# Block sums on VectorE and P1 and P2 of four column blocks ahead of the gate-up loop

## The chip, the cores and the metric

The kernel runs on one core of a Trainium2 chip. The core has a TensorE (matmuls), a VectorE, a ScalarE, a GpSimd and a SyncE (which here only issues DMAs); each runs its own instructions in order and waits for the others by semaphores. Activations and weights lie in SBUF (128 partitions), products are accumulated in PSUM. The metric is the device time of one execution in microseconds, median of several runs, lower is better.

## The reference

One encoder layer on a sequence of 1024 rows of 1024 elements, in float32: a half step of a gated feed-forward block, a mixer (latent attention and retention), and a second half step of feed-forward. The change lies in the feed-forward block alone:

```python
h = h + 0.5 * swiglu(rms_norm(h, ffn1_norm), ffn1_w_gate, ffn1_w_up, ffn1_w_down)
...                                              # mixer: attention and retention
h = h + 0.5 * swiglu(rms_norm(h, ffn2_norm), ffn2_w_gate, ffn2_w_up, ffn2_w_down)

def swiglu(x, w_gate, w_up, w_down):
    return (jax.nn.silu(x @ w_gate) * (x @ w_up)) @ w_down     # 1024 -> 2816 -> 1024
```

## The kernel before

A float32 product is made of three fast matmuls: every operand is split into a rounded part (ScalarE, a cast, line 75) and the rest (VectorE, a subtraction, line 79). `split` does both, so each operand costs one instruction on ScalarE and one on VectorE.

Each feed-forward block (`ffn`) has two stages. `gate_up` makes, for 22 blocks of 128 hidden columns (f = 0 to 21), the gate and up products. The 1024x1024 input is treated as a 2x2 matrix of blocks, and seven products in place of eight are formed from sums of blocks (Strassen's method in Winograd's form): P1 to P7, in the code `p1` to `p7`. One product is 12 matmuls of 128x512 on line 292. The inputs X of the products are six sums or blocks of the normed rows plus block 22 ("11", "21", "t2", "t3", "t1", "t4", "22"); they are made once per feed-forward block: `stats` squares rows on ScalarE and takes the reciprocal root in small steps on VectorE (lines 91 to 105), `scale` scales a row tile on VectorE (line 430), differences of rows are formed (line 456), and `turn` transposes 128x128 blocks on TensorE (line 435) and splits the result into X. The weight operands are a11, a12, a22 (raw blocks) and four sums s1 to s4, formed by `combine` and `combine4` (lines 272 to 278) on GpSimd from the raw gate and up blocks, which `fetch` brings into a ring of three raw buffers; `convert` splits an operand into one of the buffers of the pool "gu".

P1 and P2 of a block share a PSUM bank: P1 is copied out, then P2 is added to it and ScalarE takes SiLU of the sum. P6, P7, P5, P4 and P3 add further products to that; after P3 the hidden block is complete and `store` writes it to HBM. `hidden_sums` forms on GpSimd the block sums of two hidden blocks for the next stage, `fetch_down` and `down_sums` those of the down weights (through the tile "early", which holds P1 and P2 of the first blocks at the start).

Before the loop, the code is placed by a scheduler, which orders each engine's instructions by its own cost estimates; blocks 0 and 1 are done there, mixed with the transposes. From block 2 on, a hand-written list `steps` rules (`manual_schedule`): in each step one product, the conversion of the operand two steps ahead, and fetches and stores tied to certain steps. In steady state the order of a block is P7, P2, P5, P1 of the next block, P4, P6 of the next block, P3.

`down` (lines 559 to 685) runs seven passes of 11 groups of 12 matmuls (line 599) over the hidden sums and the down sums that lie in HBM; each step loads two 256 KB pieces (lines 581 and 587) and splits them (`operands`). What `gate_up` leaves over (`rest`: the last hidden block and its sums) is stored in the first pass after group 2, and the residual rows are loaded into `h` in the first pass from group 3 on. In the first feed-forward block, code that makes tables for the mixer (`tables`, from line 702) is placed by the scheduler near the end of `gate_up` and in the first pass of `down`.

Of the kernel before, what the change touches and what calls it, by code (L numbers as in the profile page):

```python
# [21 lines left out]
P = 128  # L22
# [39 lines left out]
class Layer:  # L62
# [181 lines left out]
    def gate_up(self, ctx, gain, wg, wu, wd, first):  # L244
        nc, tc, v = self.nc, self.tc, self.nc.vector
        HF = S // 2

# [19 lines left out]
        def combine(f):  # L267
# [3 lines left out]
            tt = nc.gpsimd.tensor_tensor  # L271
# [4 lines left out]
        def combine4(f):  # L276
            s = sums[f]
            nc.gpsimd.tensor_tensor(out=s[4], in0=raws["g", f][:, h2], in1=s[2], op=ALU.subtract)
# [31 lines left out]
        def p1(f):  # L310
            banks[f] = [self.ps.tile([P, HF], F32, name="dn")]
            product(banks[f][0], f, "a11", "11", True)
            kept[f, "p1"] = (early[:, 2 * f] if f < 2 else
                             take("p1"))
            nc.scalar.copy(out=kept[f, "p1"], in_=banks[f][0])  # L315

        def p2(f):
            product(banks[f][0], f, "a12", "21", False)
            kept[f, "gate1"] = (early[:, 2 * f + 1] if f < 2 else
# [56 lines left out]
        def fetch_down(m):  # L376
            b = kept["down"] = epool.tile([P, 4, 512], F32, name="early")
# [4 lines left out]
        def down_sums(m):  # L382

            b = kept.pop("down")
# [19 lines left out]
        with tc.tile_pool(name="gbc", bufs=2, reuse_waits="tile") as gpool:  # L404
            if first:
                self.load_x(1, 4)
            gbc = self.gain_rows(gpool, gain[0])
            fetch("g", 0)
            fetch("u", 0)
# [5 lines left out]
            fetch("g", 1)  # L415
# [22 lines left out]

            convert(0, "a11")
            convert(0, "a12")  # L440
            for c in range(2):
                stats(2 * c, 2)
                for t in (2 * c, 2 * c + 1):
                    scale(t)
                    turn("11", t, self.h[:, t, h1])
            for t in range(4):
                turn("21", t, self.h[:, t, h2])
            p1(0)
            combine(0)
            combine4(0)  # L450
            stats(4, 4)
            p2(0)
            convert(1, "a11")
            convert(1, "a12")

            tt = lambda eng, o, a, b: eng.tensor_tensor(out=o, in0=a, in1=b, op=ALU.subtract)
            t2s = {}
            for t in range(4):
                lo, hi = self.h[:, t], self.h[:, t + 4]
                scale(t + 4)  # L460
                t2s[t] = gpool.tile([P, 512], F32, name="t2", bufs=4)
                tt(v, lo[:, h1], hi[:, h1], lo[:, h1])
                tt(v, t2s[t], hi[:, h2], lo[:, h1])
                turn("t2", t, t2s[t])
                tt(nc.gpsimd, hi[:, h1], hi[:, h2], hi[:, h1])
                tt(nc.gpsimd, lo[:, h2], lo[:, h2], t2s[t])
            p1(1)
            for k in (2, 3):
                convert(0, k)
            for t in range(4):  # L470
                turn("t3", t, self.h[:, t + 4, h1])
            p2(1)
            p6(0)
            for t in range(4):
                turn("t1", t, self.h[:, t, h1])
            p7(0)
            for k in (1, "a22"):
                convert(0, k)
            fetch("u", 1)
            for t in range(4):  # L480
                turn("t4", t, self.h[:, t, h2])
            p5(0)
            convert(0, 4)
            combine(1)
            combine4(1)
# [3 lines left out]
        p4(0)  # L489
        p3(0)[0]()  # L490

        fetch("g", 2)
        store(0)
        convert(1, 2)
        fetch("u", 2)
        convert(1, 3)
        p6(1)
        p7(1)  # L500
        convert(1, 1)
        convert(1, "a22")
        p5(1)
        convert(1, 4)
        p4(1)
        combine(2)
        combine4(2)
        p3(1)[0]()
        fetch("g", 3)
        steps = [(p1, 2, "a11"), (p6, 2, 2)]  # L510
        for f in range(2, NF):
# [1150 lines left out]
```

## Time and profile before

| what | value |
|---|---|
| time, median of 3 runs | 2101.58 us (2097.86 to 2101.75) |
| profiled execution, its own time | 2099.66 us |
| its span from first to last instruction | 2097.4 us |
| mean granted TensorE clock | 0.979 |
| TensorE matmul busy | 1995.1 us (95%) |
| VectorE busy | 1312.0 us (63%) |
| ScalarE busy | 816.8 us (39%) |
| GpSimd busy | 747.7 us (36%) |

Shares are means over the whole span; a stage can have another limit than the mean shows. A stretch of the trace gives the busy time of each engine, the granted clock (1.00 is 2.4 GHz, 0.50 is 1.2 GHz) and the DMA share. The first feed-forward block (FFN1) begins with the execution and its `gate_up` ends near 489 us; the second (FFN2) begins near 1405 us and its `gate_up` ends near 1872 us.

### The profile page before, as it was taken

Reading aid. Unit: us, or ns where it says so; the run is one execution under the profiler, and the core shown is the slowest. Engines: PE = TensorE matmul, PEld = TensorE weight load, DVE = VectorE, ACT = ScalarE, POOL = GpSimd, SP = SyncE. Lnnn points to the kernel's source line nnn. Section 1 sums busy time; section 2 is a strip of 40 time slices with the busy share of each in tenths; the row PEclk is TensorE's granted clock in tenths of the full one; section 3 lists DMA queues with packets and bytes.
Section 4 is the critical chain, followed back from the end, with each engine's and each line's share of the span. In section 5 each row is a group of like instructions: output and inputs, shape, how many; then the busy total and the mean of one; then the engine's idle time right before and its main releaser. Section 6 shows DMA issues by size and latency. Waiting matters only on the chain. (4 is left out here: it accounts for less than half of the span.)

```text
span 2097.4 us, 28702 instructions
## 1 busy us (share of the span) xinstructions
PE 1995.1 (95%) x10776; PEld 1710.8 (82%) x10776; DVE 1312.0 (63%) x2000; ACT 816.8 (39%) x1424; POOL 747.7 (36%) x654
## 2 busy tenths in 40 slices
PE   4999999998999799999999999997999999999997
PEld 3778888886888699998878888995878888878876
DVE  8556665666555644526888888448566566565566
ACT  4322223224434331236567776224222322234444
POOL 4166666561210103312431110014376655641112
PEclk9899999999999899999999999998999999999999
DMA  4155454457666211110100000131345445468773
GB/s 150 35 167 171 161 170 150 147 170 244 232 192 191 83 41 42 51 31 1 45 12 1 1 1 21 41 131 31 134 151 173 153 148 181 146 213 283 221 229 112
DMA packets 201018, 254.66 MB, mean 121 GB/s; under 512 B 14000, under 2 KB 117680, under 8 KB 200880
## 3 DMA queue, kind: packets, MB, share of 16 engines
q1 hardware_dynamic: 199728, 250.74, 36.4%
q8 instruction: 85, 1.39, 0.3%
q10 hardware_dynamic: 1152, 2.10, 0.3%
q14 instruction: 53, 0.43, 0.1%
HBM read 180.96 MB, written 71.83 MB: 121 GB/s over the span
## 5 line engine op out<-in xcount | busy, mean ns | idle before, releaser
L292 PE MATMUL mm<-xt,gu 128*128 128x512 f32 x1584 | 387.0, 392 | 5.5 <-DVE tab L706 3.5
L292 PEld LDWEIGHTS mm<-xt,gu 128*128 128x128 f32 x1584 | 296.6, 188 | 69.8 <-ACT wd L75 5.2
L79 DVE TENSOR_TENSOR wd<-rawd,wd 128x1024 fp32r<-128x1024 f32 x143 | 189.0, 1325 | 150.1 <-ACT wd L75 149.6
L292 PE MATMUL dn<-x,gu 128*128 128x512 f32 x1056 | 260.1, 394 | 2.0 <-ACT early L315 1.4
L79 DVE TENSOR_TENSOR gu<-s,gu 128x512 fp32r<-128x512 f32 x176 | 171.3, 975 | 143.1 <-ACT gu L75 143.0
L292 PEld LDWEIGHTS dn<-x,gu 128*128 128x128 f32 x1056 | 199.0, 190 | 44.9 <-ACT early L315 2.7
L75 ACT CAST wd<-rawd 128x1024 fp32r<-128x1024 f32 x143 | 150.4, 1052 | 207.7 <-PE tp L599 71.4
L272 POOL TENSOR_TENSOR s<-raw 128x512 f32<-128x512 f32 x44 | 65.0, 1476 | 414.9 <-DMA raw<-in_ffn_w_up 218.5
L599 PE MATMUL mm<-wd 128*128 128x512 f32 x792 | 182.2, 390 | 3.1 <-DVE wd L79 2.5
L324 DVE TENSOR_TENSOR h<-mm,h 128x512 f32<-128x512 f32 x176 | 121.1, 688 | 99.8 <-PE mm L292 99.3
L599 PEld LDWEIGHTS mm<-wd 128*128 128x128 f32 x792 | 148.3, 188 | 36.1 <-DVE wd L79 4.5
L79 DVE TENSOR_TENSOR gu<-raw,gu 128x512 fp32r<-128x512 f32 x132 | 127.1, 964 | 71.3 <-ACT gu L75 71.3
L599 PE MATMUL dn<-wd 128*128 128x512 f32 x462 | 132.7, 393 | 5.2 <-DVE wd L79 5.2
L292 PE MATMUL tp<-xt,gu 128*128 128x512 f32 x528 | 132.4, 400 | 3.2 <-ACT gu L75 2.4
L354 ACT ACTIVATE h<-h 128x512 f32<-128x512 f32 x44 | 27.8, 632 | 266.4 <-DVE h L324 266.3
L599 PE MATMUL tp<-wd 128*128 128x512 f32 x462 | 130.5, 391 | 0.0
L292 PE MATMUL mm<-x,gu 128*128 128x512 f32 x528 | 127.5, 390 | 0.0
L292 PEld LDWEIGHTS tp<-xt,gu 128*128 128x128 f32 x528 | 101.6, 193 | 26.3 <-ACT gu L75 3.3
L75 ACT CAST gu<-s 128x512 fp32r<-128x512 f32 x176 | 104.5, 618 | 40.5 <-POOL s L273 31.2
L292 PEld LDWEIGHTS mm<-x,gu 128*128 128x128 f32 x528 | 98.6, 188 | 21.9 <-DVE h L324 0.9
L608 POOL TENSOR_TENSOR h<-h,u 128x512 f32<-128x512 f32 x24 | 44.0, 1866 | 195.4 <-DVE u L603 195.4
L599 PEld LDWEIGHTS dn<-wd 128*128 128x128 f32 x462 | 86.8, 189 | 25.7 <-DVE wd L79 7.8
(353 smaller groups left out, 3995.7 us busy)
## 6 DMA issues: line engine op xcount, KB each, us to landing
hid<-h SPq DMA_DIRECT2D x154, 256.0 KB, 2.7
rawd<-hid SPq DMA_DIRECT2D x154, 256.0 KB, 2.9
raw<-in_ffn_w_gate SPq DMA_DIRECT2D x44, 512.0 KB, 3.7
raw<-in_ffn_w_up SPq DMA_DIRECT2D x44, 512.0 KB, 4.1
early<-in_ffn_w_down SPq DMA_DIRECT2D x44, 512.0 KB, 4.4
wdt<-early SPq DMA_DIRECT2D x88, 256.0 KB, 2.0
rawd<-wdt SPq DMA_DIRECT2D x88, 256.0 KB, 3.4
rawd<-in_ffn_w_down SPq DMA_DIRECT2D x66, 256.0 KB, 3.3
```

What stands on the lines that cost most here:

```text
L75: nc.scalar.copy(out=hi, in_=src)
L79: eng.tensor_tensor(out=lo, in0=src, in1=hi.bitcast(F32), op=ALU.subtract)
L272: tt(out=s[1], in0=u[:, h1], in1=u[:, h2], op=ALU.add)
L292: nc.tensor.matmul(out, l[:, p], r[:, q], start=start and dt == 0 and i == 0, stop=dt == 3 and i == 2, skip_group_check=True)
L324: v.tensor_tensor(out=out, in0=ps, in1=other, op=ALU.add)
L354: nc.scalar.activation(out=g, in_=g, func=AF.Silu)
L599: nc.tensor.matmul(out, w[:, p, 0, ts_], w[:, q, 1], start=start and i == 0, stop=stop and i == 2, skip_group_check=True)
L608: nc.gpsimd.tensor_tensor(out=q, in0=q, in1=u[:, t], op=ALU.add)
```

## The change

Ahead of the loop, all block sums (of rows and, for blocks 0 and 1, of weights) are made on VectorE; before, GpSimd made them apart from two differences of rows per tile. P1 and P2 of blocks 0 to 3 are done ahead of the loop, with P6, P7 and P5 of block 0 alone; before, all seven products of blocks 0 and 1 were done there. For that, gate blocks 0 to 3 are fetched first and fetched again later together with the up blocks; "early" grows from 4 to 8 half rows and the pool "gu" shrinks from 8 to 6 buffers. The loop starts with P6 of block 1 and has five products per block for blocks 1 to 3. In the loop, stores and sums are tied to steps by a table `due`; the down sums begin at block 5, and those of the last two down blocks are made at the end. Leftover stores are spread over the first pass of `down`, two per group; the residual rows are loaded in the second pass.

```diff
-        early = epool.tile([P, 4, 512], F32, name="early")
+        early = epool.tile([P, 8, 512], F32, name="early")
-        wpool = open_pool("gu", 8, "right")
+        wpool = open_pool("gu", 6, "right")
...
-        def combine(f):
+        def combine(f, eng=nc.gpsimd):
...
+                if t == 0:
+                    p1(1)
+                elif t == 1:
+                    convert(2, "a11")
+                    convert(2, "a12")
+                    p2(1)
+                    fetch("u", 0)
+                elif t == 2:
+                    p1(2)
+                    convert(3, "a11")
+                    convert(3, "a12")
+                else:
+                    p2(2)
+            combine(0, v)
+            combine4(0, v)
+            convert(0, 2)
+            p1(3)
+            for t in range(4):
+                minus(hi[:, t, h1], hi[:, t, h2], hi[:, t, h1])
+                turn("t3", t, hi[:, t, h1])
+            convert(0, 3)
+            p2(3)
+            p6(0)
+            fetch("g", 1)
+            fetch("u", 1)
...
+            combine(1, v)
+            combine4(1, v)
...
+        steps = [(p6, 1), (p4, 0)]
+        for f in range(1, EARLY):
+            steps += [(p7, f), (p3, f - 1)] + [(p1, EARLY)] * (f + 1 == EARLY)
+            steps += [(p5, f), (p6, f + 1), (p4, f)]
...
+                elif g is p5:
+                    if f in when:
+                        at(n + 2, *down_sums(when.index(f)))
+                        if f + 1 == NF:
+                            at(n + 1, lambda: fetch_down(len(when)))
+                            at(n + 2, lambda: fetch_down(len(when) + 1))
...
         stores = hidden_sums(NF // 2 - 1)
+        for m in (len(when), len(when) + 1):
+            stores += down_sums(m)
...
-                if n == 0 and m == 2:
-                    rest()
-                if n == 0 and m > 2:
-                    nc.sync.dma_start(out=self.h[:, m - 3], in_=res[m - 3])
+                if n == 0 and m > 0:
+                    for c in rest[2 * m - 2:2 * m]:
+                        c()
+                if n == 1 and m < NT:
+                    nc.sync.dma_start(out=self.h[:, m], in_=res[m])
```

VectorE in the start of FFN1, before, from the scale of rows 4 and 5 (`h<-h,rsn,gbc`) on; `t` is a difference of rows, `xt` and `x` are the split blocks X, `gu` a split weight operand:

```order
L430 SCALAR_TENSOR_TENSOR h<-h,rsn_277,gbc 128x1024 x2
L456 TENSOR_TENSOR h<-h 128x512 x2
L456 TENSOR_TENSOR t_311<-h 128x512
L456 TENSOR_TENSOR t_324<-h 128x512
L430 SCALAR_TENSOR_TENSOR h<-h,rsn_277,gbc 128x1024
L79 TENSOR_TENSOR xt_111<-tp,xt_111 128x4x128 x2
L456 TENSOR_TENSOR h<-h 128x512
L430 SCALAR_TENSOR_TENSOR h<-h,rsn_277,gbc 128x1024
L456 TENSOR_TENSOR t_337<-h 128x512
L456 TENSOR_TENSOR h<-h 128x512
L79 TENSOR_TENSOR gu<-s,gu 128x512
```

The same place in the changed kernel, from the first block sum of weights (`s<-raw`) on:

```order
L273 TENSOR_TENSOR s<-raw 128x512
L105 SCALAR_TENSOR_TENSOR rsn_271<-rsn_271 128x4
L79 TENSOR_TENSOR gu<-raw,gu 128x512
L432 SCALAR_TENSOR_TENSOR h<-h,rsn_271,gbc 128x1024 x2
L442 TENSOR_TENSOR h<-h 128x512 x2
L442 TENSOR_TENSOR t_308<-h 128x512
L442 TENSOR_TENSOR t_333<-h 128x512
L432 SCALAR_TENSOR_TENSOR h<-h,rsn_271,gbc 128x1024
L79 TENSOR_TENSOR xt_111<-tp,xt_111 128x4x128 x2
L442 TENSOR_TENSOR h<-h 128x512
L79 TENSOR_TENSOR gu<-raw,gu 128x512
```

One block sum of weights now stands ahead of the scale and waits for the up block 0; the conversion there is of a raw block (for P1 or P2 of block 3) instead of a sum, and the other block sums follow further down the same queue.

TensorE in the start of FFN1, before, from the end of P6 of block 1 to the beginning of the loop; the names behind `<-` are the blocks X ("11" is x_103, "21" x_107, "t2" xt_111, "t3" xt_115, "t1" xt_119, "t4" xt_123, "22" x_543):

```order
L292 MATMUL tp<-xt_111,gu 128x512 x7
L292 MATMUL mm<-xt_115,gu 128x512 x11
L292 MATMUL dn<-x_103,gu 128x512 x4
L292 MATMUL mm<-xt_119,gu 128x512 x12
L292 MATMUL dn<-x_103,gu 128x512 x4
L292 MATMUL mm<-xt_123,gu 128x512 x12
L292 MATMUL dn<-x_103,gu 128x512 x4
L292 MATMUL mm<-x_543,gu 128x512 x12
L292 MATMUL tp<-xt_111,gu 128x512 x12
L292 MATMUL mm<-xt_115,gu 128x512 x12
L292 MATMUL dn<-x_107,gu 128x512 x12
L292 MATMUL mm<-xt_119,gu 128x512 x12
```

TensorE in the changed kernel, from P5 of block 0 (mixed with the transposes of "t4") into the loop; `x_611` is block "22":

```order
L437 MATMUL tp<-ident,h 128x128 x4
L293 MATMUL mm<-xt_119,gu 128x512 x6
L437 MATMUL tp<-ident,h 128x128 x4
L293 MATMUL mm<-xt_119,gu 128x512 x4
L437 MATMUL tp<-ident,h 128x128 x16
L293 MATMUL tp<-xt_111,gu 128x512 x12
L293 MATMUL mm<-xt_123,gu 128x512 x12
L293 MATMUL mm<-xt_115,gu 128x512 x12
L293 MATMUL mm<-x_611,gu 128x512 x12
L293 MATMUL mm<-xt_119,gu 128x512 x12
```

Before, P6, P7, P5, P4 and P3 of block 1 come here, with P1 of block 2 in three pieces among them, and the loop begins with P6 of block 2; now the loop begins right behind the sixteen transposes of block "22", with P6 of block 1, P4 of block 0, P7 of block 1 and P3 of block 0, and P1 and P2 of blocks 0 to 3 lie ahead of this piece.

VectorE at the end of FFN1's `gate_up`, before, where the table code (`tab`, `L704` to `L768`) is mixed in; `L324` is an addition of a product:

```order
L79 TENSOR_TENSOR gu<-raw,gu 128x512
L738 TENSOR_SCALAR tab<-tab 128x1 x4
L704 SCALAR_TENSOR_TENSOR tab<-tab 128x16
L714 TENSOR_SCALAR tab<-tab 128x16
L751 CAST tab<-tab 128x8
L758 TENSOR_TENSOR tab<-tab 128x256
L79 TENSOR_TENSOR gu<-s,gu 128x512
L763 TENSOR_SCALAR tab<-tab 128x256
L765 TENSOR_SCALAR tab<-tab 128x256
L766 TENSOR_SCALAR tab<-tab 128x256
L768 SCALAR_TENSOR_TENSOR tab<-tab 128x256
L324 TENSOR_TENSOR h<-mm,h 128x512
```

The same place in the changed kernel (lines are 18 higher in `tables`, `L325` is the addition):

```order
L79 TENSOR_TENSOR gu<-raw,gu 128x512
L756 TENSOR_SCALAR tab<-tab 128x1 x4
L722 SCALAR_TENSOR_TENSOR tab<-tab 128x16
L732 TENSOR_SCALAR tab<-tab 128x16
L79 TENSOR_TENSOR gu<-s,gu 128x512
L724 TENSOR_SCALAR tab<-tab 128x16
L325 TENSOR_TENSOR h<-mm,h 128x512
L725 RECIPROCAL tab<-tab 128x16
```

The addition of P5 (`L324`, now `L325`) has moved ahead of the wide table operations on 256 columns; it still stands behind the step that waits for the decay values' DMA.

## Rows read from the trace of the kernel before

**Rows 1.** Busy time by stretch, core 0: length, then us of each engine (instructions), granted clock, DMA share.

```profile
11.89:62.09 50.20, 27.13 (x112) 19.32 (x112) 47.17 (x64) 21.39 (x39) 30.05 (x19) 0.81 0.27 90
62.09:101.05 38.96, 38.90 (x183) 31.03 (x181) 20.31 (x31) 12.90 (x23) 1.29 (x1) 0.93 0.07 21
...
1405.60:1449.31 43.71, 26.53 (x115) 20.39 (x113) 41.22 (x53) 19.07 (x33) 30.31 (x19) 0.73 0.15 49
...
473.26:522.50 49.24, 42.29 (x169) 33.61 (x169) 33.83 (x74) 20.87 (x26) 6.74 (x11) 0.93 0.69 237
1860.10:1900.49 40.39, 38.75 (x169) 31.46 (x169) 22.02 (x21) 14.34 (x16) 7.84 (x4) 1.00 0.84 297
```

**Rows 2.** TensorE's waits over the whole span: us in total, times, longest.

```profile
PE tp L435 <- DVE t L456: 21.9, 8, 4.9
...
PE mm L292 <- DVE tab L706: 3.5, 1, 3.5
...
PE tp L292 <- ACT gu L75: 2.4, 2, 1.4
```

**Rows 3.** Timeline of TensorE: start us, us, instruction, count.

```profile
62.09 5.39 PE L292 MATMUL tp<-xt,gu 128*128 128x512 f32 x12
...
101.05 2.88 PE L292 MATMUL tp<-xt,gu 128*128 128x512 f32 x12
103.77 2.88 PE L292 MATMUL mm<-xt,gu 128*128 128x512 f32 x12
...
1487.68 2.88 PE L292 MATMUL tp<-xt,gu 128*128 128x512 f32 x12
```

**Rows 4.** VectorE by form, 11 to 62 us: count, busy us, mean ns, idle before.

```profile
L430 DVE SCALAR_TENSOR_TENSOR h<-h,rsn,gbc 128x1024 f32<-128x1024 f32 x8 | 11.9, 1521 | 0.2
L79 DVE TENSOR_TENSOR gu<-s,gu 128x512 fp32r<-128x512 f32 x7 | 7.4, 1053 | 0.0
L456 DVE TENSOR_TENSOR t<-h 128x512 f32<-128x512 f32 x4 | 6.9, 1749 | 0.0
...
L103 DVE TENSOR_TENSOR rsn<-rsn 128x4 f32<-128x4 f32 x3 | 2.2, 721 | 0.0
L103 DVE TENSOR_TENSOR rsn<-rsn 128x2 f32<-128x2 f32 x3 | 1.6, 524 | 0.1
L104 DVE TENSOR_TENSOR rsn<-rsn 128x2 f32<-128x2 f32 x3 | 1.5, 504 | 0.1
L105 DVE SCALAR_TENSOR_TENSOR rsn<-rsn 128x2 f32<-128x2 f32 x3 | 1.5, 502 | 0.1
L104 DVE TENSOR_TENSOR rsn<-rsn 128x4 f32<-128x4 f32 x3 | 1.3, 440 | 0.0
L105 DVE SCALAR_TENSOR_TENSOR rsn<-rsn 128x4 f32<-128x4 f32 x3 | 0.5, 155 | 0.0
```

**Rows 5.** VectorE by form, 60 to 104 us.

```profile
L79 DVE TENSOR_TENSOR xt<-tp,xt 128x512 fp32r<-128x512 f32 x11 | 7.5, 689 | 3.8 <-ACT xt L75 3.8
```

**Rows 6.** VectorE by form, 1405.8 to 1451 us.

```profile
L79 DVE TENSOR_TENSOR gu<-raw,gu 128x512 fp32r<-128x512 f32 x5 | 5.3, 1067 | 0.0
...
L104 DVE TENSOR_TENSOR rsn<-rsn 128x4 f32<-128x4 f32 x3 | 1.6, 519 | 0.0
...
L91 DVE TENSOR_SCALAR rsn<-ssn 128x4 f32<-128x4 f32 x1 | 1.3, 1264 | 0.0
```

**Rows 7.** Timeline of VectorE.

```profile
35.84 3.40 DVE L430 SCALAR_TENSOR_TENSOR h<-h,rsn,gbc 128x1024 f32<-128x1024 f32 x2
...
1422.91 3.60 DVE L430 SCALAR_TENSOR_TENSOR h<-h,rsn,gbc 128x1024 f32<-128x1024 f32 x2
...
1464.98 1.28 DVE L79 TENSOR_TENSOR x<-tp,x 128x512 fp32r<-128x512 f32 x2
```

**Rows 8.** Timeline of SyncE's queue and GpSimd at block 4 of FFN2.

```profile
1514.14 0.38 SPq L262 DMA_DIRECT2D raw<-in_ffn_w_up  x1
...
1521.26 1.28 POOL L272 TENSOR_TENSOR s<-raw 128x512 f32<-128x512 f32 x1 [10.18 <-DMA raw<-in_ffn_w_up]
```

More of the change, by code (lines that the diff above doesn't have):

```diff
@@ L376, in fetch_down @@
         def fetch_down(m):
-            b = kept["down"] = epool.tile([P, 4, 512], F32, name="early")
+            b = kept["down", m] = early[:, 4 * (m % 2):4 * (m % 2) + 4]
             for i in range(2):
@@ L414, in gate_up @@
                     nc.sync.dma_start(out=self.hres[t], in_=self.h[:, t])
-            fetch("g", 1)
+            fetch("g", 2)
+            fetch("g", 3)
             rs = {}
@@ L437, in turn, with minus @@
                 self.split(ps, dst[:, 0], dst[:, 1])
+            def minus(o, a, b):
+                v.tensor_tensor(out=o, in0=a, in1=b, op=ALU.subtract)
+            lo, hi, t2s = self.h[:, 0:4], self.h[:, 4:8], {}
+            for c in range(2):
+                if c == 0 and first:
+                    stats(0, 2)
+                    stats(2, 2)
+                elif not first:
+                    stats(2 * c, 2)
+                scale(2 * c)
+                scale(2 * c + 1)
+                for t in (2 * c, 2 * c + 1):
+                    turn("11", t, lo[:, t, h1])
@@ L439, in gate_up @@
             convert(0, "a11")
+            for t in range(4):
+                turn("21", t, lo[:, t, h2])
             convert(0, "a12")
[L441 to L447, printed above, removed]
             p1(0)
-            combine(0)
-            combine4(0)
             stats(4, 4)
-            p2(0)
@@ L488, in gate_up, with at, operand @@
             turn("22", t, self.h[:, t + 4, h2])
-        p4(0)
-        p3(0)[0]()
         fetch("g", 2)
-        store(0)
-        convert(1, 2)
         fetch("u", 2)
[L498 to L511, printed above, removed]
-            steps += [(p7, f, 3), (p2, f, "a12"), (p5, f, 1)]
-            steps += [(p1, f + 1, "a11"), (p4, f, "a22"), (p6, f + 1, 2)][0 if f + 1 < NF else 1:
-                                                                        3 if f + 1 < NF else 2]
-            steps += [(p3, f, 4)]
-        with tc.manual_schedule():
-            late, stores = [], []
+        names = {p1: "a11", p2: "a12", p5: 1, p6: 2, p7: 3, p4: "a22", p3: 4}
+        steps = [(p6, 1), (p4, 0)]
+        for f in range(1, EARLY):
+            steps += [(p7, f), (p3, f - 1)] + [(p1, EARLY)] * (f + 1 == EARLY)
+            steps += [(p5, f), (p6, f + 1), (p4, f)]
+        steps += [(p7, EARLY), (p3, EARLY - 1)]
+        for f in range(EARLY, NF):
+            steps += [(p7, f)] * (f > EARLY) + [(p2, f), (p5, f)] + [(p1, f + 1)] * (f + 1 < NF)
+            steps += [(p4, f)] + [(p6, f + 1)] * (f + 1 < NF) + [(p3, f)]
+        when = list(range(5, NF, 2))
+        with tc.manual_schedule():
+            late, due = [], {}
+            def at(n, *what):
+                due.setdefault(n, []).extend(what)
+            def operand(n):
+                if n < len(steps):
+                    convert(steps[n][1], names[steps[n][0]])
             for n in (0, 1):
-                convert(*steps[n][1:])
-            for n, (g, f, k) in enumerate(steps):
-                if n + 2 < len(steps):
-                    convert(*steps[n + 2][1:])
+                operand(n)
+            for n, (g, f) in enumerate(steps):
+                operand(n + 2)
                 for c in late:
```

90 lines of the change are left out of this document (37 added, 53 removed).

## Prediction

> **What bounds the kernel now.** I read the busy time by stretch first. TensorE is full nearly everywhere; the exceptions are the two starts of the feed-forward stage (FFN1 from 11.89, FFN2 from 1405.60). There TensorE worked 27.13 of 50.20 us and 26.53 of 43.71 us, while VectorE worked 47.17 and 41.22: VectorE sets the pace. In the stretch that follows (62.09 to 101.05) TensorE is full and VectorE only half busy [rows 1]. The list of waits names the same releaser: TensorE waits for the differences t that VectorE makes, 21.9 us in all [rows 2]. So the first part of a start lacks TensorE work that is ready, and the second part is TensorE work that could have stood in the first.
>
> How much is lost: the product P6 of column block 2 starts at 101.05 and at 1487.68, after 15 products, and a product takes 103.77 - 101.05 = 2.72 us [rows 3]. So the state "eleven products done" is worth 101.05 - 4 x 2.72 = 90.2, and 1476.8 in FFN2. The changed kernel reaches that state when P6 of block 1 starts, the first step of its loop; so I compare that start with 90.2 and 1476.8.
>
> Next, why VectorE is slow there. A 128x512 subtraction takes 689 ns where GpSimd is all but idle [rows 5], and two take 1.28 us, so each further one costs 0.60 [rows 7]. In FFN1's start, while GpSimd makes block sums, the same kind takes 1,749 ns (t, 4 of them) and 1,053 ns (conversions of sums, 7), the 128x1024 scale 1,521 ns (8), and steps of the reciprocal root on 128x4 or 128x2 elements, 155 ns in the undisturbed group, have means of 440 to 721 ns [rows 4]. The excess: 4 x 1.06 = 4.2, 7 x 0.36 = 2.5, 8 x (1.52 - 1.20) = 2.6 with 1.20 taken as twice 0.60, and for the five slow groups of three small steps 3 x (0.57 + 0.37 + 0.35 + 0.35 + 0.29) = 5.7. Sum 15.0 us.
>
> **The block sums on VectorE.** Per FFN VectorE gets eight sums of weights and eight differences of rows: 16 x 0.60 = 9.6 us more. GpSimd has nothing left before the loop, so 15.0 us of excess go: net 5.4 us less for VectorE. Below, all excess is taken as gone; the other bound, that none goes, is a rival.
>
> Here a rule of the Trainium skill speaks against the change: Perfetto Trace Analysis, section Optimizing Scalar/DVE Operations, says that when VectorE is saturated moving work off it, even to GpSimd, may pay. By that alone each start would get 9.6 us later. The same section warns that the two share an SBUF read port, so that such moves might not help; rows 4 side with the warning, the 155 ns steps above all.
>
> **The new order of the start.** VectorE's order now has the scale of row 4 behind six small things less to wait for. In FFN1 it started at 35.84 [rows 7]; the 5.7 us of slowed small steps lie before it, and one half-row operation fewer stands there (0.6): 29.5. In FFN2 it started at 1422.91 [rows 7]; before it go 1.1 us each at one L91 and one of three L104, 5 x 0.38 = 1.9 at the conversions [rows 6], and two conversions fewer (1.2): 1417.6. From there to the loop the order holds 53 half-row operations and 4 scales on VectorE in FFN1, 54 and 4 in FFN2: 53 x 0.60 + 4 x 1.20 = 36.6, and 37.2. Without any wait the loop is reached at 66.1 and 1454.8.
>
> TensorE's work up to there is 11 products (29.9) and 112 transposes, about 40 us. It can begin products when block 11 is split, some 6.5 us of VectorE work ahead of that scale, at 23 and 1411; so it alone would end at 63 and 1451. Both engines are nearly full, and each waits on the other in order. Splits waited 3.8 us for ScalarE's casts over 11 of them [rows 5], 0.35 each; 20 such splits in the new start make 7 us, of which I take 5 (0 to 9). In FFN1 VectorE's first sum stands ahead of the scale and waits for the up block 0, whose buffer is free only after the third gate block is converted: 1 us more (0 to 3). P6 of block 1 then starts at 72.1 and 1459.8: gains of 90.2 - 72.1 = 18.1 and 1476.8 - 1459.8 = 17.0.
>
> The weights fetched a second time, gate 0 to 3 (2 MB per FFN), cost nothing by themselves: those transfers lie in stretches where DMA is busy 0.27 and 0.15 [rows 1]. The smaller gu pool (6, not 8) costs nothing as long as P1 and P2 of the block three before are over, which by the walk above they are by 5 us or more.
>
> **The loop.** TensorE waited 2.4 us in two waits for a late conversion [rows 2], once per FFN, at P6 of block 4: the up block was issued at 1514.14 behind the down sums and GpSimd began with it at 1521.26 [rows 8], 7.1 us later. Those down sums now begin at block 5. I take half back, 1.2 (0 to 2.4). For blocks 1 to 3 the loop has five products per block, 13.6 us in place of 19.0; VectorE has 12 operations of 0.60 in that, 7.2 us, and four sums of GpSimd to meet.
>
> **Passes of down.** FFN1 takes 49.24 us from P5 of the last block to the second pass [rows 1], for 14 products' worth, 38.1: 11.1 lost. The waits show 3.5 of it at the table code (L706), and the P4 that waited needs P5's addition [rows 2]. In the new order that addition stands before the wide table operations, and the table code comes in smaller lots between the splits. I take 4 of the 11.1 back (from -2 to 8). FFN2 loses 40.39 - 38.1 = 2.3 there [rows 1]; now a fetch of the last down block stands ahead of the first loads and waits for stores: 1 us lost (0 to 3). The leftover stores follow GpSimd's last twelve sums, but loads are queued three steps (8.2 us) ahead, which covers them; the residual rows move to the second pass, where the quadrants they feed are read two passes later. Both at nothing; if the cover is gone, a load comes late by what GpSimd lacks, at most 3 us per FFN.
>
> **Sum.** 18.1 + 17.0 + 1.2 + 4.0 - 1.0 = 39.3. The profiled execution took 2099.66 us (span 2097.4), 1.9 below the median 2101.58, so the form is: 2099.66 - 39.3 = 2060.4.
>
> **Rivals.**
> *TensorE's clock stays low (the one that ends slower).* The granted clock averaged 0.81 and 0.73 over the two starts [rows 1], and after that idle time the first twelve matmuls took 5.39 us, where the later twelve took 2.88 [rows 3]. If the pieces that TensorE now gets between VectorE's splits leave it at 1.2 GHz up to the loop, its 40 us become 80: loop at 103 and 1491, 12.8 and 14.2 later than now; 2099.66 + 27.0 - 4.2 = 2122. It turns into a loss once the low clock adds more than 27 of the possible 40 us (90.2 - 63; 26 in FFN2). Against it: TensorE now has work for most of that time, and the full clock came back in the stretch where it was full (mean 0.93). At half of it: 83 and 1471, gains 7.2 and 5.8, 2083. The Trainium skill (TensorE: Matmul & The Clock Gate, on the default state being throttled until activity releases it) has the same cause; the rows agree.
> *The short early blocks starve.* A raw buffer frees only when GpSimd's fourth sum is made. Fetch 7.1, four sums of 1.28 and four hidden sums between them with a wait, about 6: 18.2, against 13.6. For: the 7.1 was seen, the 1.28 beside it [rows 8]. Against: hidden sums meet only one or two of these blocks. One block at 5 to 6 us per FFN: 2072; two: 2083.
> *VectorE stays slow without GpSimd.* If the excess is not from GpSimd's sums, 15 us per start stay: gains 3.1 and 2.0; 2090. Against it: the undisturbed 689 ns [rows 5].
> *No coupling.* The allowance of 11 us is not used and down gains 8: 2045.
>
> **Chances.** Forecast 0.47 (own range 2052 to 2070), no coupling 0.12, half-low clock 0.13, starving 0.15, VectorE slow 0.05, full low clock 0.05, gain eaten elsewhere to about nothing 0.03. The range 2046 to 2084 leaves out half of "no coupling", the slow VectorE, the low clock and the last: 0.19. Faster by over 0.2% (4 us, about what can be told from no change): 0.91; same 0.03; slower 0.06.
>
> **What would show it.** P6 of block 1 should start near 72 and 1460, with VectorE over 90% busy before and no 128x512 subtraction over 0.8 us there; GpSimd's first sum falls into the loop. Clock rows at 0.50 for 10 us or more before it show the first rival, TensorE waits at P6 of blocks 2 to 4 the second, subtractions over 1 us without GpSimd the third. The L706 wait (a new line number) should shrink below 2 us. I am wrong if that P6 starts later than 80, or if VectorE idles more than 8 us ahead of it.

## Result and profile after

| | before | after |
|---|---|---|
| median of the runs, us | 2099.77 (4 runs, 2097.86 to 2101.75) | 2075.08 (4 runs, 2073.41 to 2076.63) |
| ratio | 1 | 0.9882 [0.9865, 0.9899] |
| span of the profiled execution, us | 2097.4 | 2074.9 |
| predicted, us | | 2060 (2046 to 2084) |

The change is faster, inside the range, but by 24.7 us where 39.3 were forecast. The stretches that answer to [rows 1], by the profile after, in the columns of [rows 1]: the two starts, FFN1's from 11.89 as there and FFN2's from its first transposes, each to the loop (P6 of block 1), and the two tails, each from P5 of block 21 to the second pass of down:

```profile
11.89:70.91 59.02, 49.80 (x244) 39.31 (x244) 53.84 (x103) 33.01 (x60) 0.43 (x1) 1.00 0.34 111
1388.74:1439.28 50.54, 45.41 (x246) 35.68 (x245) 48.38 (x87) 30.24 (x54) 0.00 (x0) 0.99 0.27 83
453.84:505.85 52.01, 41.21 (x169) 32.44 (x168) 37.67 (x64) 17.13 (x18) 23.16 (x51) 0.90 0.81 273
1825.54:1878.54 53.00, 41.19 (x169) 32.96 (x168) 21.07 (x19) 15.68 (x17) 21.43 (x16) 0.87 0.79 277
```

In both starts TensorE now works for 84 and 90% of the time at a granted clock of 1.00 and 0.99 (0.81 and 0.73 in the first parts of the starts in [rows 1]), VectorE for 91 and 96%, GpSimd hardly at all. The tails took 52.01 and 53.00 us where [rows 1] has 49.24 and 40.39. So the starts won and the tails lost.

TensorE's timeline after, the places that count (start us, us, instruction, count, idle before and its releaser):

```profile
70.91 3.02 PE L293 MATMUL tp<-xt,gu 128*128 128x512 f32 x12 [0.71 <-DVE x L79]
465.40 4.82 PE L293 MATMUL mm<-xt,gu 128*128 128x512 f32 x12 [8.67 <-DVE h L325]
1439.28 4.34 PE L293 MATMUL tp<-xt,gu 128*128 128x512 f32 x12 [0.81 <-DVE x L79]
1486.32 4.82 PE L293 MATMUL tp<-xt,gu 128*128 128x512 f32 x12 [1.88 <-ACT gu L75]
1842.76 0.80 PE L616 MATMUL dn<-wd 128*128 128x512 f32 x1 [10.48 <-ACT wd L75]
```

The first and third are P6 of block 1, the fourth is P6 of block 4 in FFN2, the second is P4 of block 21 in FFN1, and the last is the first product of down in FFN2. The table of gains follows from such rows, each part as its length before minus its length after. For the loops the products are taken off: 140 of 2.72 us lie between P6 of block 1 and P5 of block 21 after (382.93 and 386.26 us), 136 between P6 of block 2 and that P5 before (372.21 and 372.42 us). The tails of before begin where P2 of block 21 ends, 0.3 and 0.9 us ahead of P5's first matmul.

| part | before | after | gain | forecast |
|---|---|---|---|---|
| FFN1, start to "eleven products done" | 90.2 | 70.9 | +19.3 | +18.1 |
| FFN1, loop, beyond its products at 2.72 | 2.3 | 2.1 | +0.2 | +0.6 |
| FFN1, P5 of block 21 to the second pass | 49.2 | 52.0 | -2.8 | +4.0 |
| between (to FFN2's first transpose, 1405.60 and 1388.74) | 883.1 | 882.9 | +0.2 | 0 |
| FFN2, start to "eleven products done" | 71.2 | 50.5 | +20.7 | +17.0 |
| FFN2, loop, beyond its products | 2.5 | 5.5 | -3.0 | +0.6 |
| FFN2, P5 of block 21 to the second pass | 40.4 | 53.0 | -12.6 | -1.0 |
| the rest | 196.9 | 196.4 | +0.5 | 0 |
| sum (of the spans) | | | +22.5 | +39.3 |

**The starts.** VectorE by form after, 10 to 70 us (count, busy us, mean ns, idle before):

```profile
L432 DVE SCALAR_TENSOR_TENSOR h<-h,rsn,gbc 128x1024 f32<-128x1024 f32 x8 | 10.0, 1281 | 0.1
L79 DVE TENSOR_TENSOR gu<-s,gu 128x512 fp32r<-128x512 f32 x5 | 3.3, 686 | 0.0
L442 DVE TENSOR_TENSOR t<-h 128x512 f32<-128x512 f32 x4 | 2.7, 689 | 0.0
L103 DVE TENSOR_TENSOR rsn<-rsn 128x4 f32<-128x4 f32 x3 | 0.5, 157 | 0.0
```

The t operations went from 1,749 to 689 ns, the small steps from several hundred to 157, the scale from 1,521 to 1,281 [rows 4].

**The tail of FFN2.** SyncE's queue, GpSimd and ScalarE before the wait of 10.48 us (start us, us, engine, line, operation):

```profile
1825.87 4.74 SPq L391 DMA_DIRECT2D wdt<-early  x4
1833.36 0.96 SPq L380 DMA_DIRECT2D early<-in_ffn_w_down  x2
1834.41 0.38 SPq L598 DMA_DIRECT2D rawd<-hid  x1
...
1828.98 1.28 POOL L390 TENSOR_TENSOR early<-early 128x512 f32<-128x512 f32 x1
...
1841.66 1.05 ACT L75 CAST wd<-rawd 128x1024 fp32r<-128x1024 f32 x1 [14.81 <-DMA rawd<-in_ffn_w_down]
```

The four stores of down block 8 wait for GpSimd's sums. The fetch of down block 10 waits until these stores are out of the half of `early` that it reuses (1833.36), and only then comes the first load of down (1834.41), 8.9 us behind P5. Its operand is converted another 7 us later; that fetch's 1 MB was issued just ahead of it. P4 was done at 1832.3. In the tail of before, the load was issued 0.2 us behind the end of P2 and converted 3.5 us later:

```profile
1860.29 0.32 SPq L581 DMA_DIRECT2D rawd<-hid  x1
1863.83 1.04 ACT L75 CAST wd<-rawd 128x1024 fp32r<-128x1024 f32 x1 [2.36 <-DMA rawd<-in_ffn_w_down]
```

**The tail of FFN1.** VectorE and GpSimd:

```profile
462.29 0.34 DVE L756 TENSOR_SCALAR tab<-tab 128x1 f32<-128x1 f32 x4 [9.26 <-POOL tab L749]
...
464.58 0.68 DVE L325 TENSOR_TENSOR h<-mm,h 128x512 f32<-128x512 f32 x1
```

```profile
460.90 1.26 POOL L389 TENSOR_TENSOR early<-early 128x512 f32<-128x512 f32 x1
462.12 0.14 POOL L749 IOTA tab<- 128x1 f32 x1
```

P5's addition (L325 at 464.58), for which P4 waits, stands on VectorE behind four 128x1 operations of the table code and a few more small ones. The four wait for GpSimd's iota (the instruction that makes the row numbers), which stands behind seven down sums in a row: four of down block 8 and three of the leftover down block 9.

### The profile page after: what moved, and what is told of

The parts are those of the page before. It is cut to its first block, busy times and chain, and to the rows that moved or that the text cites. A ratio compares the mean times of both kernels' runs of the same rounds, so it can differ in the third digit from the quotient of the medians.

```text
span 2074.9 us, 28653 instructions
## 1 busy us (share of the span) xinstructions
PE 1984.5 (96%) x10776; PEld 1705.2 (82%) x10776; DVE 1326.8 (64%) x2032; ACT 820.3 (40%) x1424; POOL 701.4 (34%) x622
## 3 DMA queue, kind: packets, MB, share of 16 engines
q1 hardware_dynamic: 208048, 254.93, 37.2%
## 5 line engine op out<-in xcount | busy, mean ns | idle before, releaser
L79 DVE TENSOR_TENSOR gu<-s,gu 128x512 fp32r<-128x512 f32 x176 | 203.6, 1164 | 135.5 <-ACT gu L75 135.4
L273 POOL TENSOR_TENSOR s<-raw 128x512 f32<-128x512 f32 x40 | 53.8, 1344 | 469.3 <-DMA raw<-in_ffn_w_up 438.6
L325 DVE TENSOR_TENSOR h<-mm,h 128x512 f32<-128x512 f32 x176 | 120.8, 687 | 62.9 <-PE mm L293 62.2
L79 DVE TENSOR_TENSOR gu<-raw,gu 128x512 fp32r<-128x512 f32 x132 | 114.3, 866 | 71.7 <-ACT gu L75 69.5
L293 PEld LDWEIGHTS mm<-x,gu 128*128 128x128 f32 x528 | 100.2, 190 | 22.5 <-DVE h L325 1.5
```

Of the source, the lines that this page charges most:

```text
L79: eng.tensor_tensor(out=lo, in0=src, in1=hi.bitcast(F32), op=ALU.subtract)
L273: tt(out=s[1], in0=u[:, h1], in1=u[:, h2], op=ALU.add)
L293: nc.tensor.matmul(out, l[:, p], r[:, q], start=start and dt == 0 and i == 0, stop=dt == 3 and i == 2, skip_group_check=True)
L325: v.tensor_tensor(out=out, in0=ps, in1=other, op=ALU.add)
```

## The experiments

Times are medians; ratios are to the kernel before, with their 95% interval. Diffs are against the changed kernel unless said otherwise.

**Who makes the sums: e1 and e2.**

```diff
-            combine(0, v)
-            combine4(0, v)
+            combine(0)
+            combine4(0)
...
-                minus(lo[:, t, h2], lo[:, t, h2], t2s[t])
+                minus(lo[:, t, h2], lo[:, t, h2], t2s[t], nc.gpsimd)
```

> The changed kernel, with the eight block sums and the eight second differences of rows (t1's and t4's operands) given back to GpSimd in the new order; nothing else. Theory (GpSimd and VectorE slow each other): VectorE has 16 x 0.60 = 9.6 us less to do per start, but the kernel before showed about 15 us of excess there, so the start gets longer by about 5.4 us: P6 of block 1 near 76 and 1450, 128x512 subtractions with means over 0.9 us, small steps well over 0.2 us, and about 2086 us in all. Rival (VectorE's number of instructions is what counts): 9.6 us fewer per start show until TensorE's own 63 us bound it: P6 of block 1 at 63 to 66, and about 2062.

Measured: 2095.54 us, ratio 0.9986 [0.9975, 0.9998]: 20.5 us worse than the changed kernel. P6 of block 1 starts at 79.53 (+8.6), in FFN2 61.4 us after its first transpose (+10.9). VectorE by form in e1, 10 to 80 us:

```profile
L79 DVE TENSOR_TENSOR xt<-tp,xt 128x512 fp32r<-128x512 f32 x16 | 10.7, 686 | 3.0 <-ACT xt L75 3.0
L442 DVE TENSOR_TENSOR t<-h 128x512 f32<-128x512 f32 x4 | 7.0, 1758 | 0.0
L79 DVE TENSOR_TENSOR gu<-s,gu 128x512 fp32r<-128x512 f32 x5 | 5.9, 1204 | 2.4 <-ACT gu L75 2.4
L103 DVE TENSOR_TENSOR rsn<-rsn 128x4 f32<-128x4 f32 x3 | 1.1, 373 | 0.0
```

With sixteen operations fewer per start VectorE got later, so the theory's direction holds and the rival falls; the loss is 1.6 and 2 times the 5.4 expected. The rows also say which operations suffer: t and the small steps, whose inputs are both in SBUF, are slow, while the split with one input in PSUM (xt from tp) stays at 686 ns. One such split, at 56.96, lies wholly beside a GpSimd sum (56.45 to 58.19) and took 0.68 us. The Trainium skill, SBUF — State Buffer, section SBUF: two separate sides, has this very distinction: a VectorE operation with two SBUF inputs takes a port pair that it shares with GpSimd, and the later one waits for the whole instruction. The trace agrees: at 31.72 a step on 128x4 elements, with a GpSimd sum of 1.29 us beside it, took 1.21 us where others take 0.16.

e2 is the other half, on the kernel before and in its order:

```diff
-            combine(0)
-            combine4(0)
+            combine(0, v)
+            combine4(0, v)
...
-                tt(nc.gpsimd, lo[:, h2], lo[:, h2], t2s[t])
+                tt(v, lo[:, h2], lo[:, h2], t2s[t])
```

> The kernel before, with its eight block sums and eight differences of each start on VectorE, in the old order; the other part of the change (P1 and P2 of four blocks first) is left out, and so is everything in the tails. Theory (sharing costs 15 us per start, the sums 9.6): each start 5.4 us shorter, so P6 of block 2 near 95.7 and 1477, about 2089 in all; the remaining gain of the change is the order. Rival (the order alone gives the gain, and the sums would cost their 9.6 us): P6 of block 2 near 110, about 2119. Other rival (the engine choice gives all of it): P6 of block 2 near 82, about 2062.

Measured: 2087.13 us, 0.9942 [0.9926, 0.9959]; P6 of block 2 at 91.13. That is 12.6 us by the sums alone, near the 10.8 expected. In the profiled execution, the fastest of the four (2081.81 us), 9.9 us lie in FFN1's start and 2.3 in FFN2's; 4.1 more lie behind FFN2's second pass, which the edit does not touch. Times to "eleven products done" (in FFN2 from the first transpose):

| | FFN1 | FFN2 |
|---|---|---|
| before | 90.2 | 71.2 |
| e2, sums alone | 80.3 | 68.9 |
| e1, order alone | 79.5 | 61.4 |
| both | 70.9 | 50.5 |

In FFN1 the parts add up (9.9 + 10.7 for 19.3). In FFN2 they give more together (20.7) than apart (2.3 + 9.8). A reading of the traces, not a test of its own: without the order TensorE has nothing else ready while it waits for the differences t. In FFN2 that wait is 10.0 us in e2 and 9.8 before; in FFN1 it fell from 12.1 to 5.6.

**The tails: e3, e4, e6, e7.** e3 takes the last fetch out of the way:

```diff
+            halves = [rpool.tile([P, D], F32, name="raw") if m > len(when) else
+                      e[:, 2 * i:2 * i + 2].rearrange("p k n -> p (k n)") for i in range(2)]
...
-                            at(n + 2, lambda: fetch_down(len(when) + 1))
+                            at(n + 1, lambda: fetch_down(len(when) + 1))
...
+        stores += last
```

> The changed kernel, with the last down block fetched into two raw buffers that are free by then (so its fetch need not wait for the stores of down block 8), one step earlier, and with the stores of down block 8's sums behind the first loads of down. Theory (the loads of down stood in SP's queue behind a fetch and stores that wait for GpSimd): TensorE's wait of 10.48 us in FFN2 for the first down operand goes, and the slow products behind it (1.4 us): second pass 12 us earlier against P5 of block 21 (about 41 us, was 53.0); in FFN1 the wait of 8.67 us is another one and stays, 1 to 2 us; about 2062 in all. Rival (the 2 MB of the two leftover blocks keep the DMA engines busy, so the loads come late in whatever order they are issued): under 4 us, 2071 or more.

Measured: 2075.06 us, 0.9876 [0.9854, 0.9899], no gain. FFN2's tail shrank from 53.0 to 45.7 (P5 1831.61, second pass 1877.29), but the operand still came late:

```profile
1831.23 0.38 SPq L604 DMA_DIRECT2D rawd<-hid  x1
...
1839.78 1.04 ACT L75 CAST wd<-rawd 128x1024 fp32r<-128x1024 f32 x1 [6.87 <-DMA rawd<-in_ffn_w_down]
```

8.5 us from issue to conversion, against 3.5 in the tail of before; here the two fetches are issued right ahead of it. So the queue's order gives 7.3 of the 12.6 us lost there; that the transfers of the fetches hold the rest, as the rival says, fits but is not shown by this run. FFN1's tail grew to 54.2: its P4 waited 11.93 us for the iota's chain, with the wide table operations now also ahead of the addition. Another 3.9 us were lost in the two loops and between FFN1 and FFN2, so that 1.2 of the 7.3 are left in the profiled execution and nothing in the median.

e4 makes the row numbers and loads the decay vectors early, in two small tiles.

```diff
+        self.row = self.small.tile([P, 1], F32, name="row", bufs=1)
+        nc.gpsimd.iota(self.row, ...
...
+            self.load_decay()
```

> The changed kernel, with the row numbers (GpSimd's iota) made at the very start and the two decay vectors loaded before the loop of FFN1, so that the table code on VectorE waits neither for GpSimd nor for SP's queue; nothing else. Theory (P5's addition of block 21 stood on VectorE behind a table instruction that waited for GpSimd's iota, which stood behind the down sums): the wait of 8.67 us at P4 of block 21 goes, but the first loads of down are late there too (first conversion at 466.96, when P4 would end near 459.5), so most of it comes back as a wait for that conversion: the second pass of FFN1 3 to 4 us earlier than 505.85, about 2072 in all. Rival (the table code alone is what is late): the whole 8.67 + 1.9 (slow products) + 1.09 us goes, 2064. FFN2 unchanged.

Measured: 2086.08 us, 0.9935 [0.9920, 0.9950], 11 us worse. Both theories miss. The table code, no longer held, ran ahead of P5's addition, from 463.66 to 475.68 (P4 waited 11.22 us), and a product of the loop took 2.80 us in place of 2.72; e11 is about that. So the next attempt has the table code later, not earlier. e7 moves the iota alone, into a part of a filler tile:

```diff
+        self.row = spare[:, 0:1]
+        nc.gpsimd.iota(self.row, ...
...
-        i_, dist = scratch(1), scratch(4)
+        i_, dist = self.row, scratch(4)
```

> The changed kernel, with GpSimd's iota alone made at the start, in a part of the filler tile; the decay loads stay. It tells which of two waits of the table code is last: if the iota alone (behind seven down sums) held VectorE, P4 of block 21 starts up to 8 us earlier than 465.40; if the decay loads on SP (issued at 458.65 behind the stores of down sums) land as late as the iota ran, VectorE waits for them until about 462, and P4 starts at 465 as before. I expect the second; no difference in the time beyond 2 us.

Measured: 2075.06 us, 0.9887 [0.9867, 0.9907], no difference, as expected. VectorE's wait has the same length with another releaser:

```profile
461.13 0.18 DVE L725 SCALAR_TENSOR_TENSOR tab<-tab 128x16 f32<-128x16 f32 x1 [9.04 <-DMA tab<-in_ret_decay_bwd]
```

The decay loads stand on SyncE's queue behind the stores of down block 8, which wait for the same GpSimd sums. e6 issues them at the second pass:

```diff
+                if extra and (n, m) == (1, 0):
+                    late = extra(tab)
+                    next(late)
```

> The changed kernel, with the row numbers made at the start in a part of the filler tile (no tile moves in SBUF), and the decay and position loads of the table code issued at the start of the second pass of FFN1's down, so that the table code cannot stand ahead of P5's addition; nothing else. Theory: P4 of block 21 follows P5 without the 8.67 us wait, but the first down operand is converted near 465 only, so TensorE waits for it instead, some 5 to 6 us: the second pass starts 4 to 5 us before 505.85, about 2070 in all. Rival (nothing comes back, the later wait takes all): 505 to 506, 2075. Other rival (all of 11 us comes back): 495, 2064.

Measured: 2074.18 us, 0.9882 [0.9867, 0.9897]; the second pass starts at 506.06, so the first rival holds. P4 follows within 0.9 us, and the whole wait is behind it:

```profile
457.51 2.99 PE L296 MATMUL mm<-xt,gu 128*128 128x512 f32 x12 [0.87 <-DVE h L328]
468.84 0.79 PE L619 MATMUL dn<-wd 128*128 128x512 f32 x1 [8.35 <-ACT wd L75]
```

FFN1 had two waits side by side, one for the table code and one for the first loads of down. Taking away the first alone is worth nothing.

**Down sums back into the loop: e5, e8, e10.**

```diff
-        when = list(range(5, NF, 2))
+        when = [5, 7, 9, 10, 11, 13, 14, 15, 17, 18, 19]
```

> The changed kernel, with the eleven down blocks fetched and summed at column blocks 5, 7, 9, 10, 11, 13, 14, 15, 17, 18 and 19, so that no down block is left for the end of gate and up; nothing else. Theory (the loads of down stand on SP behind GpSimd's last down sums and share the DMA engines with the last fetches): FFN2 from P5 of block 21 to the second pass back from 53.0 to about 40.4 us, FFN1 from 52.0 to about 45 (the iota no longer stands behind twelve sums, the table code is still ahead of P5's addition); the four blocks with hidden sums and down sums together cost GpSimd 18 us of their 19: about 2056 in all. Rival (GpSimd is too full in the loop): waits of 1 to 4 us at P6 of four blocks per FFN give back 8 to 20 us: 2064 to 2076. Other rival (e3 showed that the first loads of down take 8 us to land even when issued early, and nothing of this comes from what stands ahead of them): no gain, 2075.

Measured: 2105.02 us, 1.0022 [1.0011, 1.0033], slower than before. The theory is right on the tails, 44.2 and 39.2 us. The rival is right that the loops pay, but they took 27.5 and 25.3 us more, where it had 8 to 20 in all. SyncE and ScalarE at one such block of FFN1:

```profile
258.71 5.07 SPq L391 DMA_DIRECT2D wdt<-early  x4
263.88 0.39 SPq L263 DMA_DIRECT2D raw<-in_ffn_w_gate  x1
...
268.48 0.62 ACT L75 CAST gu<-raw 128x512 fp32r<-128x512 f32 x1 [9.17 <-DMA raw<-in_ffn_w_gate]
```

Not P6 waited but P2 (3.12 us at 269.15): its gate block is fetched behind stores that wait for GpSimd's eight sums in a row.

e8 has this edit, e6's and the one shown with e10 below.

> Three edits on the changed kernel together: the spread down blocks, the late table loads, and the fourth block sum issued on GpSimd ahead of the sums of hidden blocks (so that the raw buffer of the up block comes free earlier; in the loop TensorE waited 2.9 us at P6 of block 4 for that chain). Theory: the two tails take 40 to 42 us each (were 52.0 and 53.0) and the 2.9 us go: 23 + 2.9 = 26, about 2050. Rival (GpSimd too full in the loop): 2058 to 2070, with new waits at P6 of the blocks that have both hidden and down sums.

Measured: 2128.22 us, 1.0145 [1.0126, 1.0164]. The tails are short (39.4 and 39.3), as the theory has it, but the total is worse still, by the same kind of wait in the loops (P2 30.9 us in 12, the longest 5.7). e10 shows what the third edit does on top of e9.

e9 leaves the loop alone and moves everything that is left over behind the first loads of down (with e6's table loads):

```diff
+        return ([lambda: leftover(a), lambda: store(NF - 1)] + last + [lambda: leftover(b)] + hidden +
+                [lambda m=m, i=i: stores[m][i]() for m in (a, b) for i in range(4)])
```

> The changed kernel, with the late table loads of e6, and with the first loads of down at the head of SP's queue: the stores of down block 8 and the fetches and sums of down blocks 9 and 10 are issued between the later loads of the first pass, not before the first three. The loop is untouched, unlike in e5. Theory (both tails lose to what stands in the queues ahead of the first loads, not to the number of bytes): from P5 of block 21 to the second pass about 40 to 42 us in both FFNs (were 52.0 and 53.0): 21 to 23 us less, about 2053. Rival (the bytes count: the two leftover blocks' 2 MB and their stores now compete with the loads inside the first pass): at least half of it comes back as waits for operands of the first pass: 2064 or more.

Measured: 2079.69 us, 0.9906 [0.9891, 0.9921]. The first loads of down are no longer late (in FFN1, P4 starts at 456.37 and P3 at 461.03) and the tails are 45.8 and 47.2, 12.0 us less together. Then the second pass stands:

```profile
506.73 0.60 ACT L637 ACTIVATE u<-dn 128x512 f32<-128x512 f32 x1 [8.91 <-DMA wdt<-early]
```

```profile
509.77 0.79 PE L622 MATMUL mm<-wd 128*128 128x512 f32 x1 [5.75 <-ACT wd L75]
```

The results u1 of the first pass lie where `early` was, so ScalarE cannot write them before the last stores out of `early` have landed. From the second pass on, each FFN lost 8.1 us: 891.0 in place of 882.9 to FFN2's first transpose, 204.4 in place of 196.4 to the end. Neither theory had this. e10 is e9 with one edit more:

```diff
+                if g is p5 and f + 1 < NF:
+                    combine4(f + 1)
                 for c in due.pop(n, ()):
                     c()
...
-                    if f + 1 < NF:
-                        combine4(f + 1)
```

> e9 and the fourth block sum issued ahead of the first hidden block's sums on GpSimd (in the changed kernel that sum stood behind them, the up block's fetch behind the sum, and TensorE waited 1.42 us in FFN1 at P6 of block 4). Theory: the wait at P6 of block 4 goes in both FFNs, 2.9 us less than e9, about 2050. Rival (the hidden sums then come later and delay a store that SP's queue waits for): same as e9 or up to 3 us more.

Measured: 2097.45 us, 0.9988 [0.9978, 0.9999], 17.8 us worse than e9. The wait at P6 of block 4 did go, but in later blocks the down sums now start after that sum, their stores leave later, and the next gate block is fetched behind them (in one such block at 320.61, and P2 waited 1.34 us at 326.55). The loop of FFN1 took 391.9 us in place of 382.9. The rival holds, and it was priced far too low.

**A version that beats both: e12.** The leftover blocks go into tiles of other pools, and only the stores that the second pass reads go ahead of it (e6's table loads stay):

```diff
+        spare = ([spool.tile([P, 512], F32, name="s") for _ in range(4)],
+                 [rpool.tile([P, D], F32, name="raw") for _ in range(2)])
...
+        rest = {(0, 0): [lambda: leftover(a)], (0, 1): [lambda: leftover(b)], (0, 2): [last[1]],
...
+                (0, 9): hidden[3:] + [lambda: stores[a][1]()],
+                (0, 10): [lambda: stores[b][1]()]}
+        for k, (m, i) in enumerate((m, i) for m in (a, b) for i in (0, 2, 3)):
+            rest[1, k] = [lambda m=m, i=i: stores[m][i]()]
```

> e9, with the two leftover down blocks in tiles of the sum and raw pools (not in the early tile, over which the first pass's results u1 are laid: in e9 ScalarE waited 8.91 us for the stores out of it before it could write u1), and with only those stores ahead of the second pass that it reads; the other six of the two blocks go into the second pass, one by one. The loop is untouched. Theory (in e9 the tails were won and the loss came at the second pass's start, 5.75 and 4.99 us plus what the first pass waited): from P5 of block 21 to the second pass 43 to 46 us, no wait above 2 us at the second pass's start, and about 2062 in all. Rival (the transfers themselves are the bound of the two passes: the DMA engines moved about 400 GB/s at the end of the first pass in e9): the waits return at other operands, and it stays within 5 us of 2075.

Measured: 2054.21 us (5 runs, 2050.99 to 2057.14), ratio 0.9782 [0.9769, 0.9796]: 20.9 us better than the changed kernel, more than expected, and the rival falls. The first load of down is issued at 449.68 and 1813.50, about 3 us ahead of P5 of block 21, where the changed kernel has it 6.9 and 8.9 us behind. The two tails of e12, in the columns of [rows 1]:

```profile
452.91:492.62 39.71, 38.76 (x169) 31.38 (x168) 26.31 (x19) 15.59 (x17) 30.07 (x49) 1.00 0.91 300
1816.46:1855.70 39.24, 38.36 (x170) 31.44 (x168) 24.84 (x19) 15.79 (x18) 27.74 (x16) 1.00 0.87 295
```

39.7 and 39.2 us for 38.1 us of products. The edit changes three things at once: the order of SyncE's queue, the tiles of the leftover blocks, and six of their stores (1.5 MB) that now go into the second pass. By rate times length, the DMA engines moved 14.2 and 14.7 MB in the tails of the changed kernel and 11.9 and 11.6 MB here. So fewer bytes may have a part in the gain. That they were the only bound is not likely: in the 26 us after FFN2's first pass in e12 the engines moved 391 GB/s, and at that rate an estimate for the 14.7 MB is 38 us, not 53. For the first loads the order is enough: e9 changes it and keeps the tiles, and they are on time there. For the rest no run separates the three. Of the 26 us won in the two tails, 5.5 come back between FFN1's second pass and FFN2, 2.4 of them as waits in that pass.

**e11, the slow products of e4.** Two dead tiles and nothing else:

```diff
+        for size in (1, 16):
+            self.small.tile([P, size], F32, name=f"dead{size}", bufs=1)
```

> The changed kernel, with two dead tiles of 4 and 64 bytes per partition in the pool that e4 had put its two small tiles in; nothing uses them. In e4 a product of the loop took 2.80 us in place of 2.72 at the same granted clock of 1.00. Theory (the addresses of the operands in SBUF moved by those bytes): products of 2.80 us here too, and about 11 us more per FFN in the loop: 2095 to 2100. Rival (it came from the table code or the earlier loads of e4): 2.72, and 2075.

Measured: 2078.59 us, 0.9897 [0.9878, 0.9915]. Two products in a row of FFN1's loop in e11, and after:

```profile
85.45 2.96 PE L295 MATMUL tp<-xt,gu 128*128 128x512 f32 x12
88.25 4.12 PE L295 MATMUL mm<-xt,gu 128*128 128x512 f32 x17
```

```profile
84.65 2.88 PE L293 MATMUL tp<-xt,gu 128*128 128x512 f32 x12
87.37 2.88 PE L293 MATMUL mm<-xt,gu 128*128 128x512 f32 x12
```

2.80 us against 2.72, at a granted clock of 1.00 in both loops. So the two dead tiles are enough, without the table code. The time missed the theory's 2095 to 2100: the total rose by 3.5 us only. The loops took 9.6 and 6.7 us longer, but the tails took 47.2 and 42.9 us, 4.8 and 10.1 less. There GpSimd and SyncE were less behind: FFN2's first load of down was issued at 1837.49, 1.2 us behind P5, not 8.9.

## Why the prediction was right, and which sizes were off

1. *The starts* (18.1 + 17.0 forecast, 19.3 + 20.7 measured). The mechanism is shown by e1, e2 and the rows by form: no operation of VectorE is slowed, and it is 91 and 96% busy. The steps: the scale of row 4 was forecast at 29.5 and came at 32.79; in FFN2 1417.6, less the 16.9 us won by then, is 1400.7, and 1400.40 was measured. From there VectorE needed 38.1 and 38.9 us, where 42.6 and 42.2 were forecast. It was busy for 36.7 and 37.4 of them, as forecast (36.6 and 37.2), so of the 5 us for coupling about 1.5 are real. In that the rival "no coupling" was right. In FFN1 the late scale and the small coupling nearly cancel, which is luck. Why FFN1's scale came 3.3 us late was not tried; its first step began at 8.89 (6.98 before), and the changed order puts the gain row ahead of three rows of x on SyncE's queue.
2. *The sums against the order.* VectorE's net gain from the sums was put at 5.4 us per start. The four measurements are 9.9 and 2.3 (e2), 8.6 and 10.9 (e1). So it is not one number that a sum over excess nanoseconds gives; that it depends on what TensorE has ready is the reading above. One piece of the prediction's evidence was weak: the "undisturbed 689 ns" of [rows 5] is a split with an input in PSUM, and ten such splits took 685 ns in FFN1's start of before too, where GpSimd was busy for 30 of 50 us [rows 1]. It could not tell the two cases apart; the small steps of [rows 4], e1 and the differences t after (689 ns) can.
3. *The loop* (+1.2 forecast, -2.8 measured). The wait at P6 of block 4 was put down to down sums; it is now due to the first hidden block's sums, which stand on GpSimd ahead of block 3's fourth sum. In FFN1:

```profile
104.65 1.80 POOL L373 TENSOR_TENSOR h<-h 128x512 f32<-128x512 f32 x1
106.41 1.75 POOL L279 TENSOR_TENSOR s<-raw,s 128x512 f32<-128x512 f32 x1
112.40 1.28 POOL L273 TENSOR_TENSOR s<-raw 128x512 f32<-128x512 f32 x1 [4.25 <-DMA raw<-in_ffn_w_up]
```

   The up block is fetched when that sum frees its buffer (108.18). e10, with that sum first, has no wait at this place. The chain is the rival "short early blocks starve", at 1.4 us in FFN1 and 1.9 in FFN2 instead of 5 to 6; FFN2 paid 1.9 more for the slow product behind the wait, and 1.4 for the one at 1439.28 (granted clock 0.54 and 0.67 there).
4. *The tail of FFN2* (-1.0 forecast, -12.6 measured). This is the step that failed in size: "a fetch of the last down block stands ahead of the first loads and waits for stores: 1 us lost (0 to 3)". The wait was seen and priced at 1 us, where the first load came 8.9 us behind P5 and TensorE waited 10.48. By the rows above the price has three parts: GpSimd's sums (the last store is issued at 1830.6, 5 us behind P5), the landing of these stores (to 1833.36), and 7.25 us in place of 3.5 from the load's issue to its conversion, right behind the fetch of 1 MB. That it is this fetch which holds the load in the last part is argued, not shown.
5. *The tail of FFN1* (+4.0 forecast, -2.8 measured). P5's addition does stand ahead of the wide table operations, as forecast, but behind four small ones that need GpSimd's iota; that the down sums at the end delay GpSimd's other work was left out. The wait named L706 [rows 2] did go, and this one and the late loads took its place.
6. *Stores and residual rows at nothing.* This holds: once the first operands are there, no wait of TensorE in the first passes is above 1.1 us, and in the 54 and 61 us from the second passes on it waits nowhere. The residual rows alone were not tried.
7. *The clock.* 1.00 and 0.99 over the starts: the rival of a clock that stays low did not come true. It was lower behind the long waits of the tails: the twelve matmuls at 465.40, after 8.67 us of waiting, took 4.82 us at a granted clock of 0.57 (1.00 is 2.4 GHz, 0.50 is 1.2 GHz).
8. *The total.* 2075 lies outside the forecast's own range (2052 to 2070). The wider range, 2046 to 2084, was drawn for rivals that came true in part or not at all, and it holds the result partly by luck: against the forecast the starts gave 4.9 us more, the loops 4.0 less and the tails 18.4 less, outside the bounds given for either tail.

## What to carry to other kernels

Price a wait in an issuing queue by what the waiting entry waits for and by what is queued behind it, not by its issue time; then ask which wait is second, since removing one of two that ran side by side gave nothing (e6, e7). Moving work to an idle engine was dear where both engines read two SBUF operands (e1: 20.5 us for 32 operations). Deferred work lost what it won where its buffers were what the next stage writes (e9); in other buffers, with six of its stores put later still, it paid (e12).

## What was not expected of the hardware

Two dead tiles, together 68 bytes per partition, made the matmuls of the loop 3% slower (2.80 us for twelve, against 2.72) at the same granted clock of 1.00; those of down stayed as fast (389 ns for one in both, where those of `gate_up` went from 389 to 394). Nothing uses the two tiles, so what they can change is where other tiles lie in SBUF. Why that is slower no run here shows; e6, e7, e9 and e12 keep their small tile inside a filler tile and stay at 2.72.
